# Cross-entropy with label smoothing: the first load split over two queues by partitions in place of columns

## The chip, the core and the metric

The kernel runs on one core of one Trainium2 chip. The metric is device time in microseconds (us), the median of three runs. The profile is of one further execution; its span is a little shorter than the device time, because the device time also holds what lies before the first and after the last recorded instruction.

## What is computed

There are 256 rows of 32,000 float32 logits (32.77 MB), one integer label for each row, and a smoothing of 0.1. For each row the kernel returns one number:

```python
log_probs = logits - np.max(logits, axis=-1, keepdims=True)
log_probs = log_probs - np.log(np.sum(np.exp(log_probs), axis=-1, keepdims=True))
smooth_targets = np.full((batch, num_classes), smoothing / num_classes)
for i, label in enumerate(labels):
    smooth_targets[i, label] = 1.0 - smoothing + smoothing / num_classes
return (-np.sum(smooth_targets * log_probs, axis=-1)).astype(np.float32)
```

So a row needs three things: the sum of its logits, the logarithm of the sum of their exponentials, and the one logit that its label names. All 32.77 MB must be read once. The kernel leaves out the subtraction of the maximum, which cancels in the result.

## The kernel before

**Tiling.** Each of the 128 partitions holds two rows of the input, one after the other: partition p reads 64,000 consecutive floats. The columns are cut into tiles that all span the 128 partitions: three for the first row (8,000, 12,480 and 11,520 columns) and eleven for the second, which get smaller and smaller (8,576, 6,400, 4,608, ... down to 640), so that little work remains once the last one has arrived. In what follows tile 0 is the one of 8,000 columns, tile 1 that of 12,480, tile 2 that of 11,520, and tile 3 that of 8,576.

**Work on a tile.** The function `load` issues the transfer. `sum_logits` (L269) lets VectorE (DVE) add the two halves of the tile and accumulate the sum of the logits. `sum_exps` (L284) lets ScalarE (ACT) take the exponential of every element and accumulate those. Both wait for the whole tile. The elementwise outputs (`jd`, `ja`, `jt`) are thrown away; only the accumulated sums are used.

**Buffers.** SBUF holds three wide buffers. Tiles 0, 1 and 2 fill them first. Tile 3 then goes into the buffer of tile 0, the tiles of 6,400 and 4,608 columns into that of tile 1, and the six after them into that of tile 2; the last two have buffers of their own. A transfer into a used buffer waits until both engines are done with what was there.

**Queues.** Every transfer of logits is issued by SyncE (SP), in the order of the tiles, on SP's hardware queue, with one exception: tile 0 is divided in two. SP issues one part (L260), and ACT issues the other (L261) on its own hardware queue, so that the two queue issues at the start lie beside each other. The function `_issue_first_transfers_at_start` moves these two issues ahead of the barrier that opens the program. Tile 1 (L263) is the next instruction on SP's queue and waits for nothing, so its transfer stands in SP's queue directly behind SP's part of tile 0, while ACT's part of tile 0 stands in the other queue.

**The rest.** GpSimd (POOL) loads the labels, computes the flat addresses of the labelled logits and gathers them by two indirect transfers on a third, software queue. The first row's loss is finished while the second row streams in; TensorE transposes the two columns of losses at the end and runs some matmuls on real data shortly before, whose results nobody uses. One store (L408) writes the 256 results.

Of the kernel before, what the change touches and what calls it, by code (L numbers as in the profile page):

```python
# [131 lines left out]
def kernel(  # L132
# [7 lines left out]
    nc = tc.nc  # L140
# [3 lines left out]
    P = nc.NUM_PARTITIONS  # L144
# [23 lines left out]
    if tbl is not None:  # L168
# [10 lines left out]
    x = logits.rearrange("(p r) c -> p (r c)", r=R)  # L179
# [3 lines left out]
        out=lab[:], in_=labels.bitcast(I32).rearrange("(p f) -> p f", p=P)  # L183
    )
    rowoff = small.tile([P, R], I32, name="rowoff", tag="rowoff")
    for r in range(R):
        nc.gpsimd.iota(
            out=rowoff[:, r : r + 1],
# [6 lines left out]
        out=flat_idx[:],  # L195
# [5 lines left out]
    for r in range(R):  # L201
        nc.gpsimd.indirect_dma_start(  # L202
            out=gat[:, r : r + 1],
            out_offset=None,
            in_=logits[:],
# [21 lines left out]
    for r in range(R):  # L227
        nc.gpsimd.tensor_scalar(  # L228
            out=weighted[r],
# [10 lines left out]
    for r in range(R):  # L240
        for b in range(len(FOLLOW)):
# [3 lines left out]
            w = max(sum(parts[0]), sum(parts[1]))  # L245
# [5 lines left out]
    for t in range(sum(FOLLOW), len(WIDTHS[1])):  # L251
        w = WIDTHS[1][t]
        buffers.append(tail.tile([P, w], FP32, name=f"tail{t}", tag=f"tail{t}")[:])

    def load(w: int, col: int):
        xt = buffers.pop(0)
        if col == 0:

            h = w // 128 * 64
            nc.sync.dma_start(out=xt[:, :h], in_=x[:, :h])  # L260
            nc.scalar.dma_start(out=xt[:, h:w], in_=x[:, h:w])  # L261
        else:
            nc.sync.dma_start(out=xt, in_=x[:, col : col + w])  # L263
        return xt
# [34 lines left out]
    for t, w in enumerate(WIDTHS[0]):  # L299
        xt = load(w, col)  # L300
        col += w
        sum_logits(xt, w, sums[:, 0, t : t + 1])
        sum_exps(xt, w, sums[:, 1, t : t + 1])
# [40 lines left out]
    for t, w in enumerate(WIDTHS[r]):  # L344
        left = last - t
        xt = load(w, col)
        col += w
        part = sum_logits(
# [14 lines left out]
        elif left == 2:  # L363
            with tc.issue_after(part.ins):
                nc.vector.tensor_reduce(
                    out=done[0][:, 0:1], in_=xsum[:, : t + 2], axis=AX.X, op=ALU.add
                )
                nc.vector.scalar_tensor_tensor(
                    out=both[:],
# [7 lines left out]
        elif left < 2:  # L377
            i = 1 - left
            nc.vector.tensor_tensor(
                out=done[i + 1][:], in0=done[i][:], in1=pairs[i][:], op=ALU.add  # L380
# [20 lines left out]
        out=res[:, :, r : r + 1],  # L401
# [7 lines left out]
        out=out.rearrange("(g i) -> g i", g=1), in_=res[:].rearrange("g p r -> g (p r)")  # L409
# [36 lines left out]
```

The softmax here doesn't subtract the row's maximum and nothing guards it: scores larger than these inputs give would overflow.

## Time and profile before

| what | value |
|---|---|
| device time, median of three runs | 83.15 us (83.1 to 83.33) |
| span of the profile | 81.8 us |
| ACT busy | 57.8 us, 71% of the span |
| DVE busy | 37.0 us, 45% |
| POOL, PE busy | 10.3 us, 7.3 us |
| read from HBM | 32.77 MB, 400 GB/s over the span |
| packets on SP's queue (q1), ACT's queue (q10), the software queue (q0) | 2018, 144, 96 |

The engines' busy times are read against the span. No engine is busy throughout; the transfers are, as the line of DMA shares in the page's picture of 40 slices tells. A packet on the hardware queues is either one row of one transfer (the bytes of one partition) or one of 16 small ones of 4 bytes that close a transfer, one for each of the core's 16 DMA engines.

### The profile page before, as it was taken

Reading aid. Unit: us, or ns where it says so; the run is one execution under the profiler, and the core shown is the slowest. Engines: PE = TensorE matmul, PEld = TensorE weight load, DVE = VectorE, ACT = ScalarE, POOL = GpSimd, SP = SyncE. Lnnn points to the kernel's source line nnn. Section 1 sums busy time; section 2 is a strip of 40 time slices with the busy share of each in tenths; the row PEclk is TensorE's granted clock in tenths of the full one; section 3 lists DMA queues with packets and bytes.
Section 4 is the critical chain, followed back from the end, with each engine's and each line's share of the span. In section 5 each row is a group of like instructions: output and inputs, shape, how many; then the busy total and the mean of one; then the engine's idle time right before and its main releaser. Section 6 shows DMA issues by size and latency. Waiting matters only on the chain.

```text
span 81.8 us, 220 instructions
## 1 busy us (share of the span) xinstructions
PE 7.3 (9%) x21; PEld 5.2 (6%) x21; DVE 37.0 (45%) x37; ACT 57.8 (71%) x31; POOL 10.3 (13%) x19
## 2 busy tenths in 40 slices
PE   0000000000000000000000000000100000399701
PEld 0000000000000000000000000000000000378500
DVE  0000000990000799500099901991097757467772
ACT  5000000999300799995099998999999999999991
POOL 3200740041100000000000001992000000000000
PEclk9999999999999999999999999999999999999999
DMA  5999999999999888998699798999999999999910
GB/s 140 390 439 400 437 588 391 391 391 391 464 634 411 383 360 360 563 496 383 285 520 486 319 520 380 425 413 400 423 432 410 431 427 425 419 426 405 409 53 1
DMA packets 2258, 32.77 MB, mean 400 GB/s; under 512 B 337, under 2 KB 338, under 8 KB 1106
## 3 DMA queue, kind: packets, MB, share of 16 engines
q1 hardware_dynamic: 2018, 30.71, 88.4%
q10 hardware_dynamic: 144, 2.06, 6.0%
q0 software_dynamic: 96, 0.00, 0.1%
HBM read 32.77 MB, written 0.00 MB: 400 GB/s over the span
## 4 chain that ended last, share of the span: by engine, by line
DMA 57%; ACT 39%; issue 1%; PE 0%; DVE 0%; ACTq 0%
DMA wide<-in_logits_dram 57%; ACT ja L284 20%; ACT jt L284 19%; PE lse_t L291 0%; DVE res L400 0%; ACT lse L395 0%; ACTq L284 0%
## 5 line engine op out<-in xcount | busy, mean ns | idle before, releaser
L284 ACT ACTIVATE ja<-wide 128x8000 bf16<-128x8000 f32 (+4 forms) x5 | 40.2, 8033 | 21.2 <-DMA wide<-in_logits_dram 21.1
L269 DVE SCALAR_TENSOR_TENSOR jd<-wide 128x4000 f32<-128x4000 f32 (+11 forms) x12 | 34.5, 2876 | 39.2 <-DMA wide<-in_logits_dram 39.2
L284 ACT ACTIVATE jt<-wide 128x4608 bf16<-128x4608 f32 (+6 forms) x7 | 14.2, 2068 | 0.0
L386 PE MATMUL warm<-wide,ident 128*128 128x256 f32 x18 | 6.4, 534 | 11.8 <-DMA wide<-in_logits_dram 11.8
L386 PEld LDWEIGHTS warm<-wide,ident 128*128 128x128 f32 x18 | 4.9, 280 | 13.1 <-DMA wide<-in_logits_dram 12.0
L291 PE MATMUL loss_t<-ident,loss 128*1 128x128 f32 x1 | 0.4, 373 | 58.8 <-POOL loss L327 58.8
L316 POOL TENSOR_TENSOR lin<-acc,weighted 128x1 f32<-128x1 f32 x1 | 4.5, 4494 | 0.1
L291 PEld LDWEIGHTS loss_t<-ident,loss 128*1 128x1 f32 x1 | 0.1, 79 | 58.8 <-POOL loss L327 58.8
L311 POOL TENSOR_TENSOR acc<-sums 128x2 f32<-128x2 f32 x1 | 0.2, 192 | 16.5 <-ACT ja L284 16.5
L202 POOL DMA_INDIRECT gat<-in_logits_dram,flat_idx x2 | 2.0, 995 | 0.7 <-POOL ident masks.py:199 0.4
L330 DVE COPY res<-loss_t 1x128 f32<-1x128 f32 x1 | 0.3, 280 | 3.7 <-PE loss_t L291 3.7
L169 ACT ACT_TABLE_LOAD x1 | 1.3, 1283 | 0.9 <-PEq L427 0.9
L228 POOL TENSOR_SCALAR weighted<-gat 128x1 f32<-128x1 f32 x1 | 1.1, 1102 | 6.2 <-DMA gat<-in_logits_dram,flat_idx 6.2
L311 POOL TENSOR_TENSOR acc<-acc,sums 128x2 f32<-128x2 f32 x1 | 0.2, 193 | 12.6 <-ACT ja L284 12.6
L284 ACT ACTIVATE jt<-tail 128x704 bf16<-128x704 f32 (+1 forms) x2 | 1.5, 764 | 0.0
L284 ACT ACTIVATION_READ_ACCUMULATOR jt<-wide 128x1 f32 x7 | 1.2, 171 | 0.0
L269 DVE SCALAR_TENSOR_TENSOR jd<-tail 128x352 f32<-128x352 f32 (+1 forms) x2 | 1.0, 510 | 0.0
L269 DVE DVE_READ_ACCUMULATOR jd<-wide 128x1 f32 x12 | 1.0, 81 | 0.0
L182 POOL DMA_DIRECT2D lab<-in_labels_dram x1 | 0.8, 766 | 1.0 <-POOLq L427 1.0
L194 POOL TENSOR_TENSOR flat_idx<-rowoff,lab 128x2 int32<-128x2 int32 x1 | 0.2, 193 | 5.5 <-DMA lab<-in_labels_dram 5.5
L284 ACT ACTIVATION_READ_ACCUMULATOR ja<-wide 128x1 f32 x5 | 0.9, 173 | 0.0
L228 POOL TENSOR_SCALAR xsum<-gat 128x1 f32<-128x1 f32 x1 | 0.2, 208 | 2.6 <-DMA gat<-in_logits_dram,flat_idx 2.6
(24 smaller groups left out, 4.7 us busy)
## 6 DMA issues: line engine op xcount, KB each, us to landing
wide<-in_logits_dram SPq DMA_DIRECT2D x1, 6240.0 KB, 26.2
wide<-in_logits_dram SPq DMA_DIRECT2D x1, 5760.0 KB, 39.4
wide<-in_logits_dram SPq DMA_DIRECT2D x1, 4288.0 KB, 29.6
wide<-in_logits_dram SPq DMA_DIRECT2D x1, 3200.0 KB, 20.5
wide<-in_logits_dram SPq DMA_DIRECT2D x1, 2304.0 KB, 25.6
wide<-in_logits_dram ACTq DMA_DIRECT2D x1, 2016.0 KB, 14.0
wide<-in_logits_dram SPq DMA_DIRECT2D x1, 1984.0 KB, 11.7
wide<-in_logits_dram SPq DMA_DIRECT2D x1, 1696.0 KB
```

Of the source, the lines that this page charges most:

```text
L169: nc.scalar.add_instruction(mybir.InstLoadActFuncSet(name=nc.get_next_instruction_name(), act_func_set_id=tbl, ins=[], outs=[],))
L182: nc.gpsimd.dma_start(out=lab[:], in_=labels.bitcast(I32).rearrange("(p f) -> p f", p=P))
L194: nc.gpsimd.tensor_tensor(out=flat_idx[:], in0=rowoff[:], in1=lab[:].rearrange("p (r two) -> p r two", two=2)[:, :, 0:1], op=ALU.add,)
L202: nc.gpsimd.indirect_dma_start(out=gat[:, r : r + 1], out_offset=None, in_=logits[:], in_offset=bass.IndirectOffsetOnAxis(ap=flat_idx[:, r ...
L228: nc.gpsimd.tensor_scalar(out=weighted[r], in0=gat[:, r : r + 1], scalar1=label_weight, scalar2=None, op0=ALU.mult,)
L269: return nc.vector.scalar_tensor_tensor(out=jd[:, :h], in0=xt[:, :h], scalar=1.0, in1=xt[:, h:w], op0=ALU.mult, op1=ALU.add, accum_out=out,)
L284: return nc.scalar.activation(out=ja[:, :w], in_=xt[:, :w], func=AF.Exp, accum_out=out)
L291: nc.tensor.transpose(out=row[:], in_=column, identity=ident[:])
L311: nc.gpsimd.tensor_tensor(out=acc[:], in0=total, in1=sums[:, :, t : t + 1], op=ALU.add)
L316: nc.gpsimd.tensor_tensor(out=lin[:], in0=total[:, 0, :], in1=weighted[0], op=ALU.add)
L330: nc.vector.tensor_copy(out=res[:, :, 0:1], in_=loss_t[:])
L386: nc.tensor.matmul(warm[:], lhsT=ident[:], rhs=xt[:, i * WARM_COLS : (i + 1) * WARM_COLS], start=True, stop=True,)
```

## The change

Tile 0 is 128 partitions by 8,000 columns. Before, it is cut by columns: SP's queue carries columns 0 to 3,967 of all 128 partitions, ACT's queue columns 3,968 to 7,999 of all 128. After, it is cut by partitions: SP's queue carries all 8,000 columns of partitions 0 to 63, and ACT's queue those of partitions 64 to 127. The bytes, the destination, the two queues and the moment of issue remain. The descriptors become fewer and longer: 64 rows of 32,000 bytes on each queue in place of 128 rows of 15,872 and 128 of 16,128. The aim is a first load whose rows are whole and longer, with the two queues filling separate halves of the buffer.

```diff
         if col == 0:
 
-            h = w // 128 * 64
-            nc.sync.dma_start(out=xt[:, :h], in_=x[:, :h])
-            nc.scalar.dma_start(out=xt[:, h:w], in_=x[:, h:w])
+            h = P // 2
+            nc.sync.dma_start(out=xt[:h], in_=x[:h, :w])
+            nc.scalar.dma_start(out=xt[h:], in_=x[h:, :w])
         else:
             nc.sync.dma_start(out=xt, in_=x[:, col : col + w])
```

The order of instructions on the engines stays as it was; only the two issues of tile 0 differ in shape.

## The prediction, made before the changed kernel ran

> **What bounds the kernel now.** I read first the picture of 40 slices on the page, to see which resource is busy from start to end.
>
> ```profile
> ACT  5000000999300799995099998999999999999991
> DMA  5999999999999888998699798999999999999910
> ```
>
> One character is 2.05 us. ACT has holes in the first half (the six zeros, then 3007, then 50); DMA has none, and stays at 6 or more until its last two characters. The transfers are the bound of the first half, and ACT keeps pace in the second. Then the chain that ended last, to see how the two hand over.
>
> ```profile
> 0.91 26.20 DMA wide<-in_logits_dram
> ...
> 27.19 10.71 ACT ja L284 x2
> ...
> 37.92 20.48 DMA wide<-in_logits_dram
> ...
> 58.48 5.60 ACT ja L284 x2
> 64.08 3.82 ACT jt L284
> ```
>
> The columns are start, length, what. The first 27.11 us are one transfer, that of tile 1, issued at 0.91. From 58.48 on ACT works without a gap to the end. In between I read ACT's four big activations in the timeline, with the idle time in front of each in brackets.
>
> ```profile
> 14.24 6.87 ACT L284 ACTIVATE ja<-wide 128x8000 bf16<-128x8000 f32 x1 [12.04 <-DMA wide<-in_logits_dram]
> ...
> 27.19 10.60 ACT L284 ACTIVATE ja<-wide 128x12480 bf16<-128x12480 f32 x1 [5.99 <-DMA wide<-in_logits_dram]
> ...
> 40.76 9.80 ACT L284 ACTIVATE ja<-wide 128x11520 bf16<-128x11520 f32 x1 [2.87 <-DMA wide<-in_logits_dram]
> ...
> 50.87 7.35 ACT L284 ACTIVATE ja<-wide 128x8576 bf16<-128x8576 f32 x1 [0.21 <-DMA wide<-in_logits_dram]
> ```
>
> All four wait for their transfer. Two things follow. Tile 0 is not itself on the path: ACT is done with it at 21.2 and then idles 5.99 us for tile 1, so tile 0 may land up to 6 us later at no cost. But what delays the queue behind tile 0 delays tile 1, 2, 3 and all after them by as much, and every one is waited for. Last, whether the transfers have room to catch up: the busy time in the stretch 27 to 40 us, and the queues on the page.
>
> ```profile
> 27.00:40.00 13.00, 0.00 (x0) 0.00 (x0) 6.67 (x2) 10.70 (x2) 0.19 (x1) 1.00 1.00 431
> ```
>
> ```profile
> q1 hardware_dynamic: 2018, 30.71, 88.4%
> q10 hardware_dynamic: 144, 2.06, 6.0%
> ```
>
> The last three columns of the stretch are clock, DMA share, GB/s: the 16 DMA engines are wholly busy at 431 GB/s, 26.9 GB/s each. The 144 packets of q10 are 128 rows of tile 0 and 16 closing ones. There is no slack in the stream: a microsecond of it lost at the start is a microsecond at the end.
>
> The trace also records each packet. In tile 0 a row of 15,872 bytes took 0.59 us and one of 16,128 bytes 0.60 us, once the first rows (0.9 to 1.4 us) were over; a row of tile 1, 49,920 bytes, 1.84 us. All three are 26.9 to 27.1 GB/s, and the rows on an engine follow each other without overlap. The first row starts at 1.03, the last row of tile 0 ends at 11.97. After the first two rows of SP's queue the two queues take turns, row by row.
>
> **What the Trainium skill says.** "SBUF — State Buffer", section "Door 1: The DMA port swizzle": the partition number decides through which of 16 ports a transfer enters SBUF, about 27.2 GB/s each. Partitions 0 to 63 reach only the 8 even ports, 64 to 127 only the 8 odd ones; in a transfer of 128 partitions each DMA engine serves a port of its own. It states 196 GB/s for a load of partitions 0 to 63 and 328 for 0 to 127, both at 1 MiB. The trace agrees on the whole transfer (431 GB/s, 16 times 26.9); no transfer of 64 partitions is in it. The same page, "Can I just issue two DMAs to hit both halves?": two at once, at partitions 0 and 64, gained 6% over one. "DMA: Bandwidth & Descriptors", section "Why a DMA increments its semaphore by 16 and not by 1": 64 partitions are still spread over 16 engines, so two engines share each port. Its section "Queues, rings and completion order": an engine with work in two queues takes them in turn; the trace shows this in tile 0.
>
> **The change part by part.**
>
> Issues. One issue on each queue before and after (0.40 us on SP, 0.36 on ACT in the timeline), at the same place. Cost 0: the first row starts only at 1.03 us.
>
> Rows. Each engine had 8 rows of 15,872 and 8 of 16,128 bytes: 8 x 0.59 + 8 x 0.60 = 9.5 us. It will have 4 rows of 32,000 from each queue. At 26.9 GB/s one takes 1.19 us, and 8 x 1.19 = 9.5 us: longer rows alone gain nothing, since the short rows already ran at the same rate as those of 49,920 bytes.
>
> Ports. This is the unknown cost; no row of the trace has two engines on one port. Lower end: 0, if the two engines of a port are always in different queues, one on the even and one on the odd port. Upper end: two engines on one port at half the rate each, 2.38 us a row, 8 x 2.38 = 19.0 us in place of 9.5, so +9.5 us. The page's measurement gives about the same by another way, as an estimate: 1.06 x 196 = 208 GB/s, 4.096 MB / 208 = 19.7 us, +10.2 us. I take nearly the upper end, for this reason: all 16 engines begin with SP's queue, 1.03 to 1.63 us, and then take turns by the same rule. Two engines of a port that start d apart share it for all but d of each row, and sharing evenly leaves d as it was: nothing drives them apart. A row then takes 2 x 1.19 - d. A tile has landed when its last engine is done, so the pair with the smallest d counts; of eight pairs I guess 0.04 us from that spread of starts. 8 x (1.19 - 0.04) = 9.2 us.
>
> Tile 0's landing. 11.4 (typical end of its last rows before) + 9.2 = 20.6. Before, tile 0 was waited for until 14.24 though its last row ended at 11.97: ACT queue's closing packet comes behind one row of tile 1 (1.84 us). That stays, so ACT starts tile 0 at about 23.4. It costs nothing by itself: ACT is done at 30.4, before tile 1.
>
> Tiles 1 to 13. Their rows span 128 partitions again, 26.9 GB/s an engine, only 9.2 us later: tile 1 at 36.3, tile 2 at 50.0, tile 3 at 60.1. No new wait on buffers: tile 3 needs tile 0's buffer, free at 30.4, while the queue has work until tile 2 lands; the next needs tile 1's, free near 47, before tile 3 lands.
>
> POOL's small transfers. They take turns with the longer rows and land some us later, but the gathered logits (17.5 and 21.3 before) are first used at 51.06. Cost 0, hidden under the activations.
>
> Sum: 83.15 + 9.2 = 92.35, say 92.3 us.
>
> **The rivals.**
>
> (a) The queues fall out of step, so that one engine of each pair writes even and the other odd ports. Full rate, tile 0 lands as before, and the stream is as long: 83.15, not slower. For it: both halves of the ports have work at all times, 16 engines and 16 ports. Against: the common start, the same rule for all, and the page's 6%.
>
> (b) Partly out of step: SP's first two rows, taken alone as in the trace of before, cost 2 x 1.19 = 2.4 us and the rest between nothing and 7. 85.5 to 91, middle 88.
>
> (c) A half goes to eight engines, SP's to one eight and ACT's to the other. Each has 8 rows of 1.19 us, at full rate. But ACT's eight have tile 1's rows in SP's queue from the start, and in turns need 1.5 + 8 x (1.19 + 1.84) = 25.8 us until tile 0 is complete. Tiles 1 to 3 land as before, ACT is late instead: 26 + 6.95 + 10.8 + 10.0 + 7.4 = 61.2, where it needs to begin the tile of 6,400 columns at 58.48. +2.7 us, 85.9. Against: the page's rule of 16 engines.
>
> (d) Sharing a port costs more than half the rate: above 93.8. Nothing in the profile speaks for it; the page's 208 GB/s gives 93.3.
>
> (e) Fewer, longer rows save part of the slow beginning (the first rows' extra 0.3 to 0.8 us): at most 0.4 us, 82.75. Against: that is latency before the first byte, not cost by row.
>
> **How the numbers follow.** Sharing nearly throughout, 91 to 93.8: 0.66. (b) 0.12, (c) 0.06, (a) 0.08, (d) 0.04, (e) 0.04. The time is that of the likeliest, 92.3. The range from 85.5 to 93.8 takes in sharing, (b) and (c), 0.84, and leaves out (a), (d) and (e), 0.16. Slower: 0.66 + 0.12 + 0.06 + 0.04 = 0.88; same: 0.08; faster: 0.04.
>
> **What would show it right or wrong.** Right: in the picture of slices the GB/s are near 215 up to about 20 us and above 400 afterwards; rows of 32,000 bytes take 2.2 to 2.4 us in the packet records; ACT starts tile 0 near 23, tile 1 near 36.3, tile 2 near 50, with idle times before tile 2 and tile 3 as before (2.9 and 0.2). Rows of 1.19 us with tile 0 at about 14 would show (a); rows of 1.19 us with tile 0 near 26 and tile 1 still near 27 would show (c); a mixture of both lengths (b). The prediction is wrong if tile 1 lands before 30, or if it lands at 36 and the end doesn't follow.

## The result, and the profile after

| | before | after |
|---|---|---|
| device time, median of six executions | 83.14 us (83.08 to 83.33) | 92.75 us (92.5 to 93.09) |
| span of the profile | 81.8 us | 91.2 us |
| ACT busy | 57.8 us | 57.8 us |
| DVE busy | 37.0 us | 37.0 us |

The changed kernel takes 1.1154 times as long (95% interval 1.113 to 1.1178). In what follows two executions that lay over 1.5% above the fastest of their kernel, 96.05 us of e5_two_pieces and 92.05 us of e6_four_pieces, are left out of the ratios; the profile of e6_four_pieces is of the latter. The engines do the same work in the same busy time; 9.4 us more of the span are waiting. Where they arise is seen in the picture of 40 slices of the changed kernel, one character for 2.28 us:

```profile
ACT  3200000000699400999970999999999999999991
DMA  9999998988988898798796998899999899999930
GB/s 211 239 211 225 225 226 197 225 261 351 482 351 351 373 657 345 324 586 384 324 627 261 482 467 361 376 494 404 427 404 461 384 447 412 426 417 421 411 157 0
```

The line of DMA shares alone would show nothing: it is as full as before. Only the GB/s below it differ. The first eight slices, 18 us, move 197 to 239 GB/s, and from the tenth on the values are back around 400 (single slices jump, because a packet's bytes are put down to one slice). The stretches from 1 to 12 us and from 49 to 67 us of the changed kernel tell it with two numbers, after the line of the kernel before from 1 to 12 us; the last two columns are DMA share and GB/s:

```profile
1.00:12.00 11.00, 0.00 (x0) 0.00 (x0) 0.00 (x0) 1.20 (x1) 3.57 (x8) 1.00 1.11 445
```

```profile
1.00:12.00 11.00, 0.00 (x0) 0.00 (x0) 0.00 (x0) 1.28 (x1) 1.15 (x4) 1.00 1.06 233
...
49.00:67.00 18.00, 0.00 (x0) 0.00 (x0) 10.80 (x4) 16.63 (x3) 4.90 (x3) 1.00 1.00 430
```

A share of 1.06 at 233 GB/s, where the kernel before had 1.11 at 445: a packet that moves at half speed (rows of 2.31 us in place of 1.19) counts as busy for twice as long. The queues on the page say the same of ACT's part of tile 0, whose bytes are nearly what they were:

```profile
q10 hardware_dynamic: 80, 2.05, 10.3%
```

64 rows and 16 closing packets now take 10.3% of 16 engines' span, where 128 shorter rows took 6.0% of a shorter span. What it does to ACT, from the timeline of the changed kernel:

```profile
23.60 6.87 ACT L284 ACTIVATE ja<-wide 128x8000 bf16<-128x8000 f32 x1 [20.84 <-DMA wide<-in_logits_dram]
...
36.57 10.60 ACT L284 ACTIVATE ja<-wide 128x12480 bf16<-128x12480 f32 x1 [6.01 <-DMA wide<-in_logits_dram]
...
50.15 9.80 ACT L284 ACTIVATE ja<-wide 128x11520 bf16<-128x11520 f32 x1 [2.88 <-DMA wide<-in_logits_dram]
...
60.27 7.35 ACT L284 ACTIVATE ja<-wide 128x8576 bf16<-128x8576 f32 x1 [0.23 <-DMA wide<-in_logits_dram]
```

All four begin 9.36 to 9.40 us later than before, each after the same idle time as before (6.01, 2.88 and 0.23, against 5.99, 2.87 and 0.21), except the first. The delay arises in tile 0 and is carried on unchanged.

The chain of waits of the changed kernel needs care:

```profile
0.12 23.39 DMA wide<-in_logits_dram
...
23.60 6.97 ACT ja L284 x2
...
30.59 29.59 DMA wide<-in_logits_dram
```

It goes from ACT's part of tile 0 over ACT's exponentials to the transfer of tile 3, which was issued at 30.59 when they gave the buffer free. Read literally, the exponentials of tile 0 would now be on the path. They aren't: in the packet records the rows of tile 2, ahead of tile 3 in SP's queue, run until 49.66, so a free buffer at 24 would have brought tile 3 no earlier. The chain follows events, and a transfer's issue isn't the moment at which its queue reaches it: tile 3's first row starts at 49.17.

### The profile page after: what moved, and what is told of

The parts are those of the page before. It is cut to its first block, busy times and chain, and to the rows that moved or that the text cites. A ratio compares the mean times of both kernels' runs of the same rounds, so it can differ in the third digit from the quotient of the medians.

```text
span 91.2 us, 220 instructions
## 1 busy us (share of the span) xinstructions
PE 7.1 (8%) x21; PEld 5.0 (6%) x21; DVE 37.0 (41%) x37; ACT 57.8 (63%) x31; POOL 9.5 (10%) x19
## 3 DMA queue, kind: packets, MB, share of 16 engines
q10 hardware_dynamic: 80, 2.05, 10.3%
## 4 chain that ended last, share of the span: by engine, by line
DMA 58%; ACT 39%; issue 1%; PE 0%; DVE 0%; ACTq 0%
DMA wide<-in_logits_dram 58%; ACT ja L284 22%; ACT jt L284 17%; PE lse_t L291 0%; DVE res L400 0%; ACT lse L395 0%; ACT lse L325 0%; ACTq L284 0%
## 5 line engine op out<-in xcount | busy, mean ns | idle before, releaser
L228 POOL TENSOR_SCALAR weighted<-gat 128x1 f32<-128x1 f32 x1 | 0.2, 234 | 6.5 <-DMA gat<-in_logits_dram,flat_idx 6.5
## 6 DMA issues: line engine op xcount, KB each, us to landing
wide<-in_logits_dram SPq DMA_DIRECT2D x1, 2304.0 KB, 25.5
wide<-in_logits_dram ACTq DMA_DIRECT2D x1, 2000.0 KB, 23.4
```

Of the source, the lines that this page charges most:

```text
L228: nc.gpsimd.tensor_scalar(out=weighted[r], in0=gat[:, r : r + 1], scalar1=label_weight, scalar2=None, op0=ALU.mult,)
```

## The experiments

The theory (P): two DMA engines that write into one side of partition 64 share a port of SBUF and get half the rate each. Its rivals: that the place or shape of what is read is slow (H), that rows of 32,000 bytes are slow (L), that taking turns between two queues is slow (Q). Every edit below replaces the two issues of tile 0. Of the transfers that an edit gives to a queue, only the first stands ahead of the opening barrier. Where the number of transfers changes, the semaphores are cleared by two instructions in place of one at the end. The packet records name no engine; row durations are medians of the 16 rows, one for each engine, that a queue carries side by side. Rows "in succession" follow a row of their own queue, rows "in turns" one of the other queue.

**A port for each engine (e1_middle).**

```diff
-            nc.sync.dma_start(out=xt[:h], in_=x[:h, :w])
-            nc.scalar.dma_start(out=xt[h:], in_=x[h:, :w])
+            nc.sync.dma_start(out=xt[32:96], in_=x[32:96, :w])
+            nc.scalar.dma_start(out=xt[:32], in_=x[:32, :w])
+            nc.scalar.dma_start(out=xt[96:], in_=x[96:, :w])
```

> SP loads partitions 32 to 95 (64 of them, half below and half above 64), ACT 0 to 31 and then 96 to 127, whole rows of 32,000 bytes as in the changed kernel. If two DMA engines share an SBUF port when all 64 partitions lie on one side of 64: SP's rows get a port per engine and take 1.19 us, ACT's rows still share and take 2.3 to 2.5 us; tile 0 needs 4 x 1.19 + 4 x 2.4 = 14.4 us in place of 18.95, so 92.75 - 4.6 = 88.2 us. If it is reading 64 rows (the HBM side), the row length, or two queues in turns that is slow: SP's rows take 2.3 us too, and the time stays at 92.7.

Measured: 88.64 us, ratio to before 1.065 (1.0629 to 1.0671). Here ACT's queue came first. Its first two rows took 2.22 and 2.51 us, with all engines below partition 32. SP's second row, with all engines in partitions 32 to 95, took 1.19 us: 64 partitions, whole rows, at full speed. SP's other rows, which had ACT's rows beside them, took 1.65 to 1.88, so tile 0 needed 15.5 us (1.25 to 16.79, by typical engines) in place of the expected 14.4. The change of speed is seen in the first slices (2.18 us each) of this kernel's GB/s:

```profile
GB/s 235 235 206 264 235 397 206 469 366 366 367 596 481 389 338 359 613 381 338 529 400 456 299 504 488 380 388 458 412 414 431 405 461 403 421 419 418 408 101 0
```

L falls, and so does a slowness of 64 partitions as such.

**Reading or writing (e8_read_middle, e9_write_middle).** e1_middle moved both what is read and what is written; these two move one each. In both, tile 0 holds the first 8,000 columns of other input rows in some of its partitions.

```diff
# e8_read_middle
+            nc.sync.dma_start(out=xt[:64], in_=x[32:96, :w])
+            nc.scalar.dma_start(out=xt[64:], in_=x[64:, :w])
# e9_write_middle
+            nc.sync.dma_start(out=xt[32:96], in_=x[:64, :w])
+            nc.scalar.dma_start(out=xt[:32], in_=x[64:96, :w])
+            nc.scalar.dma_start(out=xt[96:], in_=x[96:, :w])
```

> Into partitions 0 to 63, SP reads the input rows that belong to partitions 32 to 95; ACT fills 64 to 127 as in the changed kernel. Tile 0 then holds the wrong input rows in half of its partitions; nothing else changes. If the destination's partitions decide (ports): as the changed kernel, rows of 2.3 to 2.5 us, 92.7 us. If the place that is read decided in the run with partitions 32 to 95: SP's rows 1.19 us when alone, about 88.

> The reverse: into partitions 32 to 95, SP reads the input rows of partitions 0 to 63, and ACT fills 0 to 31 and 96 to 127 from the others. Tile 0 again holds the input rows in another order. If the destination decides: SP's rows 1.19 us when all engines are at them, 88.6 us. If the place that is read decides: rows of 2.3 to 2.5 us, 92.7 us.

Measured: 92.59 us (ratio 1.1138, 1.1098 to 1.1178) and 88.69 us (1.0641, 1.0616 to 1.0667). The stretch from 1 to 12 us, first of the one that reads the middle, then of the one that writes it:

```profile
1.00:12.00 11.00, 0.00 (x0) 0.00 (x0) 0.00 (x0) 1.28 (x1) 1.15 (x4) 1.00 1.05 233
```

```profile
1.00:12.00 11.00, 0.00 (x0) 0.00 (x0) 0.00 (x0) 1.28 (x1) 1.15 (x4) 1.00 1.05 279
```

The first has the 233 GB/s of the changed kernel, the second the 279 that e1_middle also has. The destination's partitions decide; H falls as the cause. A detail stays open: e9_write_middle differs from e1_middle only in what is read, and its second row from SP took 1.36 us, not 1.19, the other three 1.54 to 1.70. What is read thus shifts single rows, but not the time (88.69 against 88.64).

**One queue (e2_one_queue).**

```diff
-            nc.scalar.dma_start(out=xt[h:], in_=x[h:, :w])
+            nc.sync.dma_start(out=xt[h:], in_=x[h:, :w])
```

> Both partition halves on SP's queue, one after the other; ACT's queue is unused. Sharing of ports: still two engines on a port, 8 rows of 2.3 to 2.5 us, 92.7 to 93.7 us; the higher end if taking turns between the two sides saves the 0.2 us a row by which rows in turns (2.31) were shorter than rows of one queue in succession (2.5) in the changed kernel. If taking turns between two queues is the cost: rows of 1.19 us and about 83.2.

Measured: 93.53 us, ratio 1.1239 (1.1216 to 1.1262). ACT's queue is gone, and rows take 2.51 us, except the first (2.38) and the fifth (2.47). Q falls: turns between the queues don't cost, they save 0.2 us a row, for in the changed kernel rows in turns took 2.31 us (SP's last 2.41), and those in succession 2.49 to 2.51. In the changed kernel queue and side of partition 64 change together. The fifth row here is the first of the other side, on the same queue: a change of side alone gave 0.04 us. No run lets two queues take turns on one side.

**Long rows alone (e3_whole).**

```diff
-            nc.sync.dma_start(out=xt[:h], in_=x[:h, :w])
-            nc.scalar.dma_start(out=xt[h:], in_=x[h:, :w])
+            nc.sync.dma_start(out=xt[:], in_=x[:, :w])
```

> Tile 0 as one transfer of all 128 partitions on SP's queue, rows of 32,000 bytes, ACT's queue unused. Sharing of ports: a port per engine, rows of 1.19 us, 83.0 to 83.4 us as before the change. If rows of 32,000 bytes are slow in themselves: 2.3 us a row and about 92.7. ACT starts tile 0 at about 12 rather than 14.2, since no closing packet waits behind a row of tile 1; that should be worth nothing.

Measured: 83.38 us, ratio 1.0027 (1.0012 to 1.0041); rows 1.19 us. From its timeline:

```profile
12.16 6.87 ACT L297 ACTIVATE ja<-wide 128x8000 bf16<-128x8000 f32 x1 [10.06 <-DMA wide<-in_logits_dram]
27.09 10.60 ACT L297 ACTIVATE ja<-wide 128x12480 bf16<-128x12480 f32 x1 [7.97 <-DMA wide<-in_logits_dram]
```

Tile 0 is there 2.08 us earlier than in the kernel before, tile 1 at the same time (27.09 against 27.19), and the end doesn't move to the good: tile 0's own landing is off the path, as the idle time in front of tile 1 says.

**More engines on a port (e4_sixteen, e7_sixteen_one_queue).** Tile 0 in eight transfers of 16 partitions, on both queues in the first, on SP's alone in the second. If 16 partitions are served by half as many ports as 64 on one side, P makes a row twice as long: 2 x 2.31 to 2 x 2.51 us.

```diff
+            h, g = P // 2, 16
+            for p in range(0, h, g):
+                nc.sync.dma_start(out=xt[p : p + g], in_=x[p : p + g, :w])
+                nc.scalar.dma_start(out=xt[h + p : h + p + g], in_=x[h + p : h + p + g, :w])
# e7_sixteen_one_queue: nc.sync in place of nc.scalar
```

> Tile 0 as eight transfers of 16 partitions, four on each queue, rows of 32,000 bytes. [...] rows of 4.6 to 5.0 us, tile 0 in 37 to 40 us in place of 18.95, 92.75 + 18.5 to 21 = 111 to 114 us if the sharing of ports is right. If only the count of 64 rows or the division over two queues matters: rows of 2.3 us and 92.7 to 94.

> As the eight transfers of 16 partitions, but all on SP's queue, so the two sides of 64 are never in turns. Four engines on a port at the 25.5 GB/s that two engines got without turns (2 x 32,000 bytes in 2.51 us): rows of 5.0 us, 8 x 5.0 = 40.2 us in place of 18.95, about 113.5 to 114. If the rate with four engines is not the port's but a queue's: 4.34 us a row as with turns, and 108.5.

Measured: 108.52 us (ratio 1.3066, 1.3025 to 1.3108) and 108.65 us (1.3044, 1.3006 to 1.3082). The stretch from 12 to 20 us, all of it tile 0, of e4_sixteen and then of e7_sixteen_one_queue:

```profile
12.00:20.00 8.00, 0.00 (x0) 0.00 (x0) 0.00 (x0) 0.00 (x0) 0.00 (x0) 1.00 1.11 128
```

```profile
12.00:20.00 8.00, 0.00 (x0) 0.00 (x0) 0.00 (x0) 0.00 (x0) 0.28 (x2) 1.00 1.13 128
```

The order of size is as P wants it, the amount isn't. Rows took 4.34 and 4.38 us in place of 4.6 to 5.0, so e4_sixteen lies below what was expected. e7_sixteen_one_queue met the second of its numbers, 108.5, but not for the reason given there: a queue alone isn't the limit, for in e3_whole SP's queue carried rows of 1.19 us. Nor is the number of transfers, for e6_four_pieces (below) also has eight and takes 91.32 us.

The expectation of e7_sixteen_one_queue also misread its own edit. The loop issues a piece of the lower half and then one of the upper, so the two sides of partition 64 do alternate, row by row, on the one queue. The two runs differ only in the queue of the upper half, and 4.34 against 4.38 us says that with the same alternation of sides a second queue is worth 0.04 us a row. A run whose pieces of 16 partitions stay on one side was not made.

If four engines share a port all the time, it passed 4 x 32,000 bytes / 4.38 us = 29.2 GB/s, more than the 25.5 of two engines without turns (2 x 32,000 / 2.51) or the 26.9 of one (32,000 / 1.19). Either one fixed rate of a port is too simple, or four engines were not on it throughout: in e7_sixteen_one_queue the rows of one transfer begin up to 2 us apart (7.89 to 9.85), so an early engine is already at the next transfer, on the other side. This stays open.

**More turns (e5_two_pieces, e6_four_pieces).** As the changed kernel, with each half cut into k pieces by columns, k = 2 and 4.

```diff
+            h, g = P // 2, w // k
+            for c in range(0, w, g):
+                nc.sync.dma_start(out=xt[:h, c : c + g], in_=x[:h, c : c + g])
+                nc.scalar.dma_start(out=xt[h:, c : c + g], in_=x[h:, c : c + g])
```

> As the changed kernel, but each partition half goes in two pieces of 4,000 columns: 8 rows of 16,000 bytes on each queue for each engine, so twice as many turns between the queues. If each turn saves about 0.2 us whatever the row's length (rows in succession 2.51 us, rows in turns 2.31): a row takes 1.25 - 0.2 = 1.05 us, 16 x 1.05 = 16.8 us in place of 18.95, 90.6 us. If two engines simply get 27.7 GB/s from a port when they take turns, in proportion to the bytes: rows of 1.155 us, 18.5 us, about 92.5.

> As the one with two pieces, with four of 2,000 columns: 16 rows of 8,000 bytes on each queue for each engine. A fixed saving of 0.2 us a turn: 0.63 - 0.2 = 0.43 us a row, 32 x 0.43 = 13.8 us in place of 18.95, 87.5 us. In proportion to the bytes: rows of 0.58 us and about 92.5.

Measured: 93.75 us (92.98 to 96.05, ratio 1.124, 1.1157 to 1.1323) and 91.32 us (90.53 to 92.05, ratio 1.0942, 1.0866 to 1.1017). For the first both expectations missed. Its rows show part of why. SP's rows in succession took 1.25 us and in turns mostly 1.06 to 1.11, so a turn saves 0.14 to 0.19 us there too: less than the fixed 0.2, more than the 0.1 in proportion. But ACT's rows began only at 5.62, when SP had done four rows, and ended at 24.64, long after SP's at 16.39; by then they ran beside rows of tile 1, whose first took 2.58 us in place of 1.84. The two queues didn't stay side by side. That this lost what the turns had saved fits, but no run shows it apart. e6_four_pieces lies between its two expectations. In its profile most rows in turns took 0.48 to 0.51 us in place of the 0.63 that 2.51 / 4 gives, so a turn saved 0.12 to 0.15: again neither fixed nor in proportion. Tile 1's first rows took 2.47 us in place of 1.84 here too. How its time divides was not settled.

## Why the prediction was right

**What bounds the kernel.** Right (though the first character of its line of DMA shares is a 5, not 6 or more: the first row starts only at 1.03 us). The stream of transfers has no slack, and tile 0's landing has 6 us of it. e3_whole shows the second on its own: 2.08 us earlier, and no gain. Between the last row of tile 1 (26.73 before, 36.06 after) and of tile 2 (40.33, 49.66) the delay stays at 9.33 us.

**Issues, costed at 0.** Slightly wrong. In the timelines SP's issue takes 0.55 us in place of 0.40, and the first row starts at 1.33 in place of 1.03. It goes with 64 partitions: e2_one_queue has 0.55 and 1.34, whereas e3_whole (128 partitions) has 0.40 and 1.04, and e7_sixteen_one_queue (16) 0.39 and 1.02. What in an issue of 64 takes longer is not shown. By typical engines the first row starts 0.36 later.

**Rows, costed at 0 by their length.** Right: 1.19 us in e3_whole.

**Ports, costed at 9.2 us.** Right that writing 64 partitions of one side nearly doubles a row, and nearly right in size, with a formula for the row that didn't hold. From the typical start of the first row to that of tile 1's first row the changed kernel needs 20.46 - 1.49 = 18.97 us, the one before 11.47 - 1.13 = 10.34: +8.63. That the destination's partitions are the cause is shown by e1_middle, e8_read_middle and e9_write_middle. The prediction had 8 x (2 x 1.19 - 0.04) = 18.7 and 9.5. So it was off most on the side of before: it took all rows there at the full rate, but SP's first two took 1.04 and 0.68 us in place of 0.59. The formula, a row of 2 x 1.19 - d with d the distance between two engines' starts, isn't borne out. The 16 engines began ACT's first row between 5.89 and 6.87, the last of them 0.2 after the one before it, and all 16 took 2.30 to 2.32 us. With d = 0.2 for that last engine the formula gives at most 2.18. What shortens a row is the turn between the queues, by 0.2 us for every engine. Why it does so is open; the change of side alone, in e2_one_queue, gave 0.04. The trace doesn't record which engine writes which partition. That two engines share one port is thus the page's account, which the runs fit; no run tells it from another limit that goes with the side of partition 64.

**Tiles 1 to 13, costed at 0.** Slightly wrong: the rest of the 9.33, +0.34 us, counted to its last engine (by typical engines tile 1's rows took 35.79 - 20.46 = 15.33 us against 26.27 - 11.47 = 14.80, +0.53). Tile 1's first rows took 2.30 us in place of 1.85, beside the last rows of tile 0, and some later ones 1.88. Together 0.36 + 8.63 + 0.34 = 9.33. The predicted 9.2 came out close because two small costs left out (0.36 and 0.34) about made up for a third that was 0.57 too large. In that the closeness is luck, and so is the guess of 0.04 us for d: the rows averaged 18.97 / 8 = 2.37 us, near its 2.34, but for another reason. The span grew by 9.4, the median time by 9.6.

**Landing of tile 0, buffers, small transfers.** Right. The typical last row ends at 20.47, against 20.6 predicted. ACT waits 2.6 us beyond the last row's end (21.00) for the closing packet, and starts at 23.60 against 23.4 predicted. The gathered logits arrive at 29.09 and 32.82 and are first used at 60.44.

**The rivals.** (a), falling out of step, didn't occur in the changed kernel; rows stayed at 2.3 to 2.5 us to the end. (b) would have shown some rows near 1.19 us, (c) all of them. Neither was there. ((b)'s terms add up to 83.15 + 2.4 + 7 = 92.6, not 91, so its band and that of full sharing overlap; (c)'s sum gives 25.7, not 25.8.) (d), more than half the rate lost, holds for rows in succession (2.51 against 2 x 1.19 = 2.38), which is what e2_one_queue adds; its 93.53 us still lies below the 93.8 that (d) names. (e), gaining at the beginning, turned out the other way for the start, which came 0.36 us later. Yet the long first row isn't seen again: in the changed kernel it took 2.25 us, not more than the 2.51 of the second.

**The skill's figures.** In the Trainium skill, "SBUF — State Buffer", section "Door 1: The DMA port swizzle", the 196 GB/s for partitions 0 to 63 at 1 MiB compares with 16 x 32,000 / 2.51 us = 204 GB/s here. The 6% for two transfers at once, in section "Can I just issue two DMAs to hit both halves?", compares with 2.51 / 2.31, 9% by rows, and with 5% over tile 0 (19.90 us in e2_one_queue, 18.97 in the changed kernel). That section's sentence that only one transfer over all 128 partitions reaches every port isn't borne out by e1_middle: partitions 32 to 95 ran at the full rate of 128, rows of 1.19 us.

## What to carry to other kernels

When a load is divided, look at which partitions each piece writes: here a row took twice as long (2.3 to 2.5 us against 1.19) when a piece lay on one side of partition 64, and not when it was partitions 32 to 95 or all 128. Dividing by columns leaves the partitions whole, as the kernel before does. A DMA share near 1 says that packets are under way, not that they are fast, so read it with the GB/s beside it. And a first load that nobody waits for can still set the end if the stream behind it has no slack.

## What the runs showed that was not expected

- The issue of a transfer of 64 partitions holds its queue longer than one of 128 or 16 (0.55 against 0.40 and 0.39 us on SP), and its first row starts 0.3 us later.
- Rows that take turns between two queues, one on each side of partition 64, are faster than rows in succession (2.31 against 2.51 us), and a change of side on one queue gave only 0.04 us.
- With transfers of 16 partitions rows took 4.34 to 4.38 us, less than twice the 2.31 to 2.51 of 64 on one side. Whether a port passes more with four engines (29.2 GB/s, if they share it throughout) is not shown.
